# A hybrid conv and forgetting-attention layer in float32 on one core: low parts move from GpSimd to VectorE before the attention, and some small matmuls are queued with a margin

## Chip, cores and metric

The kernel runs on one core of one Trainium2 chip. The metric is the device time of one execution in microseconds (us). Kernels are compared by their medians, runs of both being taken on the same chip.

A core has five engines, each of which works through its own queue in order: TensorE (PE, with its weight loads as PEld), VectorE (DVE), ScalarE (ACT), GpSimd (POOL) and SyncE (SP), which here only issues DMAs.

## The reference

One layer with post-norm is applied to 1024 new prompt tokens and to 32 tokens of a running stream with 512 cached positions; model width 1024. What matters here, cut down:

```
p = x @ w_in                      # GLU pair | q | k | v | forget logits | branch gates
u = a * sigmoid(b)
y = depthwise_causal_conv(u, width 31) + b_dw          # 512 channels
y_conv = silu(layer_norm(y)) @ w_conv_out
logf = log_sigmoid(p_f + b_f);  c = cumsum(logf)
o = softmax(q k / 8 + c_q - c_k, causal) v             # 8 heads of 64
m = sigmoid(g_conv) * y_conv + sigmoid(g_attn) * (o @ w_attn_out)
x1 = layer_norm(alpha * x + m @ w_o)
x2 = layer_norm(alpha * x1 + relu(x1 @ w_up)^2 @ w_down)
```

Everything is float32, and the keys, values, log forget values and last conv inputs are outputs too.

## The kernel before

Features lie on partitions, tokens run along the free axis: 1056 tokens in three chunks of 352. Each float32 operand is split into two float32r tiles: a high part (a copy by ACT, or a cast by DVE) and a low part, the subtraction of the high part from the operand (`tt(lo, a, hi, SUB)`). A float32 product is then three passes on PE: high by high, high by low, low by high. The weights are streamed in tiles of 128 x 1024, loaded in halves (`raw`), and split by `Weights.split`: `whi` on ACT, `wlo` by a subtraction on POOL (on DVE only for the first two halves). Raw halves and split tiles have four buffers each.

The stages up to the attention are: the GLU pairs (8 weight tiles); the values (4 tiles); queries and keys (8 tiles); and the first 6 of 16 gate tiles (`ps_g`, 72 matmuls each). Beside them three background streams run:

- `conv()`: on DVE, four channel tiles `ca` of 128 x 1086, each made by one `TENSOR_SCALAR` and 30 taps (`SCALAR_TENSOR_TENSOR ca<-u,prm,ca`). Then, in three chunks c0 to c2 of 362 tokens, a layer norm over channels in `norm_rows`: `total` adds the four tiles, a matmul with a constant matrix spreads the mean (`ps_mu_c`), DVE subtracts it, ACT squares, `total` adds the squares, a second matmul gives the variance (`ps_var_c`), then a square root, a reciprocal, and per tile `done`: a product with 1/std, a sigmoid (`csig`), a product, a high part on ACT (`csh`) and a low part (`csl`). Both go to DRAM (`s_s`).
- `forget()`: the log sigmoid of the forget logits on small tiles (ending with `logf` and `lfs`), running sums by four matmuls (`ps_cum`) and a transpose (`ps_cumt`).
- `x_stream()`: the inputs.

What sets the order is `Issue`. It keeps a rough clock per engine (`t`) from a cost for every operation, and nothing of it is known to the chip: the order of issue is simply the order of each engine's queue. A stream yields what it waits for, and `service`, called after every group of six matmuls, goes on with a stream when `due(need)` is not after the modelled PE clock. For a list of tiles, `due` is the modelled time at which they stand ready. For taps the need is `("dve", 1500)`: a tap is issued when DVE's modelled clock is less than 1500 ns ahead of PE's. At the end of the stage `I.flush()` issues whatever the streams still hold.

After that the pools of the stage close and those of the attention take their place. `load_head` loads operands of a head (k1, q1, k2, q2, v) over SP's queue; k1 of the first head lies where tiles `ca0` and `ca1` lay. The remaining gates are a filler between the attention's matmuls. Merge, output projection and feed-forward follow.

Of the kernel before, what the change touches and what calls it, by code (L numbers as in the profile page):

```python
# [17 lines left out]
P = 128  # L18
# [37 lines left out]
WARM = 19  # L56
GB = 2
# [21 lines left out]
class Issue:  # L79
    """Issues instructions and keeps a rough clock for each engine. Every engine works in the order of  # L80
    issue, so work that stands ready is put in front of work that would wait: `fill` and `service`."""
# [32 lines left out]
    def due(self, need):  # L114
        if callable(need):
            return 0.0 if need() else 1e12
        if isinstance(need[0], str):
            return max(self.t[e] for e in need[:-1]) - need[-1]
        return max(max(self.ready(a), self.free.get(a.tensor.name, 0.0)) for a in need)
# [19 lines left out]
    def finish(self, last):  # L139
        """issues what is left of a background stream and of those before it in its group"""  # L140
# [11 lines left out]
    def drain(self):  # L152
        """issues all background streams: the oldest that can go on, or else the first that can"""
# [6 lines left out]
    def pick(self, n, bias=0.0):  # L160
        """the engine that would be through with a tensor_tensor first"""
        pool, dve = (max(self.t[e], self.t["pe"] - 500) for e in ("pool", "dve"))
        return "pool" if pool + n * 1.97 + 150 + bias < dve + n * 1.01 + 80 else "dve"
# [74 lines left out]
class Slots:  # L238
    """A tile pool whose slots the clock knows"""
# [24 lines left out]
def hybrid_layer(ctx: ExitStack, tc, io):  # L264
# [15 lines left out]
    # ---- scratch in DRAM  # L280
# [20 lines left out]
    # ---- weights: streamed, split in two float32r parts that add up to the float32 exactly  # L301
# [10 lines left out]
    class Weights:  # L312
        def __init__(self):
            self.raw, self.parts, self.taken, self.done, self.halves = [], [], 0, 0, 0

# [7 lines left out]
        def split(self):  # L323
# [8 lines left out]
            tt(lo, raw, f32(hi), SUB, "dve" if i < 2 else "pool")  # L332
# [26 lines left out]
    def mm3(ps, terms, late=False, low=False):  # L359
        """ps = sum of w.T x over terms; each float32 product as hi hi + hi lo + lo hi"""  # L360
# [17 lines left out]
    # ---- layer norm of one block of tokens, features on the partitions of several tiles: 1/std and  # L378
    # the centred rows in place; a background stream whose steps come when their operands stand ready
# [16 lines left out]
    def norm_rows(pl, psl, tiles, mean, tag, n, s, engs, done):  # L396
        yield [s]
# [9 lines left out]
        yield [s]  # L407
# [7 lines left out]
    # sixteen rows of tiles: the inputs, then what the merge reads, then the residual and hidden units  # L415
# [11 lines left out]
    def gates(tiles, banks, staging, tag, bufs, xh_read=None):  # L427
        """the gates before their sigmoid; xh_read is called with the last tile's products of xh through"""
# [27 lines left out]
    # =============================================================== projections, convolution  # L456
    with pool("conv") as pv_, pool("a") as pa, pool("pa", space=PSUM) as psa:
# [40 lines left out]
        # products of ones, read by nobody, bring the tensor engine to its full clock as the inputs arrive  # L498
# [61 lines left out]
        def conv():  # L560
# [7 lines left out]
            for c in range(3):  # L568
                cs = slice(c * CC, (c + 1) * CC)
                tiles = [ca[j][:, cs] for j in range(NJ)]  # L570
                s = total(pv_, tiles, f"m{c}", CC, ("dve", "dve", "pool", "pool"))

                def done(rstd, c=c, cs=cs, tiles=tiles):
                    for j, y in enumerate(tiles):
# [8 lines left out]
                        tt(lo[:, j, :], y, f32(hi[:, j, :]), SUB, "pool")  # L583
                    for dst, src in ((s_s[0], hi), (s_s[1], lo)):
# [3 lines left out]
                        else:  # L588
# [5 lines left out]
                                     ("dve", "dve", "pool", "pool"), done)  # L594

        # ---- log sigmoid of the forget logits and its running sums
        logf = pa.tile([P, 9, H], F32, name="logf")

        def forget():
# [21 lines left out]
            yield [logf, lfs]  # L621
# [10 lines left out]
            yield [cum]  # L632
# [8 lines left out]
        # the first tiles go chunk by chunk, as the inputs arrive  # L641
# [17 lines left out]
        # ---- values, tokens on partitions  # L659
        for half in range(2):  # L660
            ws = [W.take() for g in range(2)]
            for t in range(9):
# [15 lines left out]
                tt(vs[:r, :, DH:P], vv, f32(vs[:r, :, 0:DH]), SUB, "pool")  # L678
# [12 lines left out]
        # ---- queries (times -1/8) and keys, features on partitions  # L691
        for m in range(4):
            for name in "qk":
                w = W.take()
                for c in range(NCH):
# [7 lines left out]
                    tt(lo, a, f32(hi), SUB, "pool")  # L703
# [23 lines left out]
    # =============================================================== attention, branch gates  # L727
    with pool("b") as pb, pool("pb", space=PSUM) as psb:
# [21 lines left out]
        # the first products of the merge, as the rows of the inputs come free  # L750
# [28 lines left out]
        # operands of one head: [kh; kh] on [qh; ql] and [kl; c, 1] on [qh; 1, -c] add up to all of  # L779
        # -(q k / 8 + c_q - c_k)  # L780
# [17 lines left out]
        # two heads of the running stream: their cached keys and values are split on the chip  # L798
# [87 lines left out]
        class Rows:  # L886
            """128 query rows of one head against their keys"""
# [56 lines left out]
        class Stream:  # L944
            """the new queries of two heads of the running stream against cached and new keys"""
# [93 lines left out]
    # =============================================================== merge, output projection, FFN  # L1039
# [62 lines left out]
    def run_sum(cs, m, s, tag, eng="dve"):  # L1102
        """adds tile m of a block of tokens to the running sum over features"""
# [12 lines left out]
    def squares(sq, t, total, nth, n, tag):  # L1116
        """squares one more tile and adds the square before it to the running sum"""
# [15 lines left out]
    def norm_out(cs, tag, s, emit, need=()):  # L1133
        """layer norm of a block of tokens in place, a background stream as well"""
# [66 lines left out]
    with pool("h") as ph:  # L1201
# [28 lines left out]
        def down_first(wd, cs):  # L1230
            """the first tiles, with what the newest hidden units add put last"""
# [44 lines left out]
        def output(cs, new=False):  # L1276
            """where a block of tokens puts its results: in place, or two tiles at a time"""
# [21 lines left out]
        # the last tokens go through the last hidden units block by block, with the weights kept  # L1299
# [28 lines left out]
        # the last block: the mean over its first tile is taken off as soon as it is known, which leaves  # L1328
# [134 lines left out]
```

## Time and profile before

| | us |
|---|---|
| median of 3 runs | 1587.16 |
| lowest and highest | 1586.59, 1590.54 |
| span of the profiled execution | 1585.9 |
| PE busy in it | 1506.2 |
| DVE, ACT, POOL busy | 911.8, 487.4, 655.2 |

The record of the profiled execution gives its span from the first to the last instruction; what lies around the span is taken as the difference to the median, 1.3 us.

How to read it: slices are 40 equal parts of the span with the busy share in tenths. In rows of groups the numbers behind `|` are busy us and mean ns of one, then the idle time just before and what ended it. In rows in order of time: start, us, engine, line, operation, output<-inputs, shapes, count, and in brackets idle time before and its releaser. In the list of waits: total us, times, longest. `ps_` names a PSUM tile; buffer numbers are left out.

### The profile page before, as it was taken

The page shows a single profiled execution, that of the slowest core. Times are in us where ns is not written, and L with a number is a line of the kernel's source. Part 1 is how long each engine was busy: PE and PEld are TensorE (multiplying, and loading weights), DVE is VectorE, ACT ScalarE, POOL GpSimd, SP SyncE. Part 2 cuts the span into 40 slices and gives each one's busy share as a digit, 9 for nine tenths or more (in the row PEclk, how much of TensorE's full clock was granted, in tenths as well). Part 3 has the DMA queues.
Part 4 walks back from the last instruction along what each step waited for, and adds up shares of the span by engine and source line. Part 5 has one row for each costly group of instructions (what it writes and reads, how often), then busy time and mean ns, then how long its engine had stood idle before and what let it go on. Part 6 is the DMA issues. An engine that isn't in the chain of part 4 may idle for free.

```text
span 1585.9 us, 24681 instructions
## 1 busy us (share of the span) xinstructions
PE 1506.2 (95%) x9524; PEld 1476.5 (93%) x9524; DVE 911.8 (57%) x1385; ACT 487.4 (31%) x1048; POOL 655.2 (41%) x557
## 2 busy tenths in 40 slices
PE   9999598699999999999899999999999999999985
PEld 8999598698989999899899999999999999999984
DVE  4799999653656654864887243333424333342588
ACT  4211211453656655433554121111111111111133
POOL 2436576633445533657765222222222222222346
PEclk9999699899999999999999999999999999999998
DMA  6214443437555557626531111111111111114412
GB/s 199 69 46 137 134 136 125 151 114 219 152 142 147 146 150 269 210 87 190 154 96 54 47 47 41 54 41 50 44 47 47 41 54 41 54 41 140 153 37 73
DMA packets 113731, 165.56 MB, mean 104 GB/s; under 512 B 19146, under 2 KB 71626, under 8 KB 113614
## 3 DMA queue, kind: packets, MB, share of 16 engines
q1 hardware_dynamic: 113614, 163.99, 33.6%
q8 instruction: 75, 1.23, 0.3%
q14 instruction: 42, 0.34, 0.1%
HBM read 120.38 MB, written 43.54 MB: 103 GB/s over the span
## 4 chain that ended last, share of the span: by engine, by line
PE 67%; DVE 7%; issue 2%; ACT 1%; DMA 1%; POOL 1%; SPq 0%; DVEq 0%; ACTq 0%; POOLq 0%
PE ps_dn L202 22%; PE ps_up L202 22%; PE ps_g L202 8%; PE ps_yc L202 3%; PE ps_o L202 2%; PE ps_s L202 2%; PE ps_pv L202 2%; PE ps_tr L206 2%; PE ps_yo L202 2%; DVE acc L231 2%; DVE lnvar_n L223 2%; DVE acc L223 0%; DVE yg L223 0%; DVE rstd_n L235 0%; DMA g_s<-gt 0%
## 5 line engine op out<-in xcount | busy, mean ns | idle before, releaser
L223 POOL TENSOR_TENSOR wlo<-raw,whi 128x512 fp32r<-128x512 f32 (+1 forms) x262 | 381.8, 1478 | 605.6 <-ACT whi L214 598.7
L214 ACT ACTIVATE whi<-raw 128x512 fp32r<-128x512 f32 (+1 forms) x264 | 151.9, 623 | 396.9 <-issue 337.6
L202 PE MATMUL ps_dn<-hh,whi 128*128 128x352 f32 x768 | 249.3, 325 | 0.0
L202 PE MATMUL ps_dn<-hl,whi 128*128 128x352 f32 x768 | 247.8, 323 | 0.8 <-DVE hl L223 0.8
L202 PE MATMUL ps_dn<-hh,wlo 128*128 128x352 f32 x768 | 248.0, 323 | 0.0
L223 DVE TENSOR_TENSOR acc<-ps_dn,acc 128x352 f32<-128x352 f32 x168 | 87.8, 523 | 194.5 <-PE ps_dn L202 194.5
L231 DVE SCALAR_TENSOR_TENSOR ca<-u,prm,ca 128x1086 f32<-128x1086 f32 x120 | 197.7, 1648 | 2.5
L223 DVE TENSOR_TENSOR r<-r 128x352 f32<-128x352 f32 x96 | 52.5, 547 | 184.7 <-ACT r L214 184.7
L202 PEld LDWEIGHTS ps_dn<-hl,whi 128*128 128x128 f32 x768 | 144.5, 188 | 1.3 <-DVE hl L223 1.0
L202 PEld LDWEIGHTS ps_dn<-hh,whi 128*128 128x128 f32 x768 | 144.3, 188 | 0.5 <-DVE acc L223 0.2
L202 PEld LDWEIGHTS ps_dn<-hh,wlo 128*128 128x128 f32 x768 | 144.4, 188 | 0.0
L202 PE MATMUL ps_g<-xh,whi 128*128 128x352 f32 x384 | 132.4, 345 | 0.7 <-ACT gt L214 0.6
L214 ACT ACTIVATE r<-ps_up 128x352 f32<-128x352 f32 x96 | 44.5, 463 | 259.8 <-PE ps_up L202 253.6
L202 PE MATMUL ps_g<-xh,wlo 128*128 128x352 f32 x384 | 124.1, 323 | 0.0
L202 PE MATMUL ps_g<-xl,whi 128*128 128x352 f32 x384 | 121.9, 323 | 0.0
L223 DVE TENSOR_TENSOR hl<-r,hh 128x352 fp32r<-128x352 f32 x96 | 84.0, 875 | 3.3
L223 DVE TENSOR_TENSOR tl<-ps_tr,th 128x512 fp32r<-128x512 f32 (+2 forms) x96 | 51.2, 553 | 57.9 <-ACT th L214 56.0
L202 PE MATMUL ps_up<-x_0h,whi 128*128 128x352 f32 x256 | 82.9, 324 | 0.0
L202 PE MATMUL ps_up<-x_1h,wlo 128*128 128x352 f32 x256 | 82.4, 322 | 0.0
L202 PE MATMUL ps_up<-x_0h,wlo 128*128 128x352 f32 x256 | 82.4, 322 | 0.0
L202 PE MATMUL ps_up<-x_1h,whi 128*128 128x352 f32 x256 | 82.4, 322 | 0.0
L202 PE MATMUL ps_up<-x_0l,whi 128*128 128x352 f32 x256 | 82.3, 322 | 0.0
(283 smaller groups left out, 3834.6 us busy)
## 6 DMA issues: line engine op xcount, KB each, us to landing
raw<-in_w_in_dram SPq DMA_DIRECT2D x64, 256.0 KB
raw<-in_w_up_dram SPq DMA_DIRECT2D x64, 256.0 KB
raw<-in_w_down_dram SPq DMA_DIRECT2D x64, 256.0 KB
raw<-in_w_o_dram SPq DMA_DIRECT2D x48, 256.0 KB
g_s<-gt SPq DMA_DIRECT2D x48, 176.0 KB
yg<-g_s SPq DMA_DIRECT2D x48, 176.0 KB
xr<-in_x_dram SPq DMA_DIRECT2D x12, 352.0 KB
xr<-in_x_dram SPq DMA_DIRECT2D x24, 176.0 KB
```

The costliest lines, as they stand in the source:

```text
L202: self.nc.tensor.matmul(ps, lhsT=w, rhs=x, start=start, stop=stop)
L206: self.nc.tensor.transpose(ps, x, ident)
L214: self.nc.scalar.activation(out, in_, func, **kw)
L223: (self.nc.vector if eng == "dve" else self.nc.gpsimd).tensor_tensor(out, a, b, op)
L231: self.nc.vector.scalar_tensor_tensor(out, a, s, b, op0, op1)
```

## The change

Three things change. Up to the attention all low parts and sums of `total` are made by DVE instead of POOL, which is left with filling constants (memsets); `W.engine` is set back to POOL before the attention. A need may now be `(MARGIN, [tiles])`, which is due 3000 ns of the modelled clock after the tiles stand ready. The two products of each conv norm and the products of the running sums have such needs. Comments are taken out as well.

```
+MARGIN = 3000.0
...
     def due(self, need):
         if callable(need):
             return 0.0 if need() else 1e12
+        if isinstance(need[0], float):
+            return self.due(need[1]) + need[0]
...
     class Weights:
         def __init__(self):
+            self.engine = "dve"
...
-            tt(lo, raw, f32(hi), SUB, "dve" if i < 2 else "pool")
+            tt(lo, raw, f32(hi), SUB, self.engine)
...
     def norm_rows(pl, psl, tiles, mean, tag, n, s, engs, done):
-        yield [s]
+        yield (MARGIN, [s])
         mu = psl(f"mu_{tag}")[:, :n]
         mm(mu, mean, s, True, True)
...
         s = total(pl, sq, f"v{tag}", n, engs)
-        yield [s]
+        yield (MARGIN, [s])
...
-                s = total(pv_, tiles, f"m{c}", CC, ("dve", "dve", "pool", "pool"))
+                s = total(pv_, tiles, f"m{c}", CC, ("dve",) * 4)
...
-                        tt(lo[:, j, :], y, f32(hi[:, j, :]), SUB, "pool")
+                        tt(lo[:, j, :], y, f32(hi[:, j, :]), SUB)
...
-                                     ("dve", "dve", "pool", "pool"), done)
+                                     ("dve",) * 4, done)
...
-            yield [logf, lfs]
+            yield (MARGIN, [logf, lfs])
...
-            yield [cum]
+            yield (MARGIN, [cum])
...
-                tt(vs[:r, :, DH:P], vv, f32(vs[:r, :, 0:DH]), SUB, "pool")
+                tt(vs[:r, :, DH:P], vv, f32(vs[:r, :, 0:DH]), SUB)
...
-                    tt(lo, a, f32(hi), SUB, "pool")
+                    tt(lo, a, f32(hi), SUB)
...
+    W.engine = "pool"
     with pool("b") as pb, pool("pb", space=PSUM) as psb:
```

How the order moves, at two places. The first is PE's queue at the mean product of chunk c1, before, in the middle of the gates (`ps_g1`, `ps_g2`: second and third gate tile; line 202 is the helper that issues matmuls):

```order
L202 MATMUL ps_g1_2_78_2936<-xh7_101,whi21_2480 128x352
L202 MATMUL ps_g1_2_78_2936<-xl7_109,whi21_2480 128x352
L202 MATMUL ps_g1_2_78_2936<-xh7_101,wlo21_2481 128x352
L202 MATMUL ps_mu_c1_79_2974<-lns_dve_m1_2910,mean_c_193 128x362
L202 MATMUL ps_g2_0_80_2993<-xh0_94,whi22_2596 128x352
L202 MATMUL ps_g2_0_80_2993<-xl0_102,whi22_2596 128x352
```

The same product in the changed kernel, on PE at the end of the stage (`ps_g5` is its last gate tile, `ps_g6` the attention's first filler):

```order
L205 MATMUL ps_g5_2_89_3272<-xl7_109,whi25_2885 128x352
L205 MATMUL ps_g5_2_89_3272<-xh7_101,wlo25_2886 128x352
L205 MATMUL ps_mu_c1_91_3347<-lns_dve_m1_3343,mean_c_193 128x362
L205 MATMUL ps_var_c1_92_3365<-lns_dve_vc1_3361,mean_c_193 128x362
L205 MATMUL ps_mu_c2_93_3402<-lns_dve_m2_3398,mean_c_193 128x362
L205 MATMUL ps_var_c2_94_3420<-lns_dve_vc2_3416,mean_c_193 128x362
L205 MATMUL ps_g6_0_3493<-xh0_94,whi26_2986 128x352
```

The mean product of c1 moved from place 1774 of PE's queue to 2062, and the three products after it, which had some 30 to 100 gate matmuls between them, stand directly behind it. The mean product of c0 moved from 1640 to 1994, its variance product from 1671 to 2049, and the first running-sum product from 1131 to 1161.

The second place is DVE's queue in the changed kernel, where the norm of chunk c0 ends and that of c1 begins (line 226 is the helper of subtractions and additions, 234 that of `SCALAR_TENSOR_TENSOR`):

```order
L234 SCALAR_TENSOR_TENSOR ca3_208<-ca3_208,prm_86,rstd_c0_3287 128x362
L234 SCALAR_TENSOR_TENSOR ca3_208<-ca3_208,prm_86,csig0_3_3336 128x362
L226 TENSOR_TENSOR csl0_3320<-ca3_208,csh0_3319 128x362
L226 TENSOR_TENSOR lns_dve_m1_3343<-ca0_205,ca1_206 128x362
L226 TENSOR_TENSOR lns_dve_m1_3343<-lns_dve_m1_3343,ca2_207 128x362
L226 TENSOR_TENSOR lns_dve_m1_3343<-lns_dve_m1_3343,ca3_208 128x362
L226 TENSOR_TENSOR ca0_205<-ca0_205,ps_mu_c1_91_3347 128x362
```

The low part `csl0` and the second and third addition were on POOL before, beside DVE's queue; now they stand in it, ahead of the subtraction of the mean.

## The prediction

> **What bounds the kernel now.** I read the page first, then the list of what TensorE (PE) waits for up to 420 us, then stretches of 20 us.
>
> ```profile
> span 1585.9 us, 24681 instructions
> ...
> PE 1506.2 (95%) x9524; PEld 1476.5 (93%) x9524; DVE 911.8 (57%) x1385; ACT 487.4 (31%) x1048; POOL 655.2 (41%) x557
> ...
> PE   9999598699999999999899999999999999999985
> ...
> PEclk9999699899999999999999999999999999999998
> ```
>
> PE is busy for 95% of the span; its holes stand in slices 5, 7 and 8 of 40, all before the attention, and the granted clock drops there too. Nearly all of the idle time has two owners (us in total, times, longest), with one more row at the attention's first scores:
>
> ```profile
> PE ps_mu_c L202 <- DVE lns_dve_m L223: 19.6, 2, 18.4
> PE ps_cum L202 <- DVE lfs L218: 19.4, 1, 19.4
> PE ps_s L202 <- DMA q<-qh_s: 1.9, 1, 1.9
> ```
> ```profile
> 186.50 0.66 PE L202 MATMUL ps_cum<-logf,cst 128*128 128x64 f32 x2 [19.43 <-DVE lfs L218]
> 290.02 1.54 PE L202 MATMUL ps_mu_c<-lns_dve_m,mean_c 128*128 128x362 f32 x2 [18.40 <-DVE lns_dve_m L223]
> ```
> ```profile
> 180.00:200.00 20.00, 13.50 (x66) 13.51 (x67) 18.86 (x46) 3.35 (x8) 11.06 (x7) 0.65 0.47 153
> 240.00:260.00 20.00, 20.00 (x127) 20.00 (x127) 19.79 (x15) 4.41 (x9) 13.03 (x7) 1.00 0.38 134
> 280.00:300.00 20.00, 9.98 (x50) 9.25 (x51) 13.92 (x16) 7.02 (x12) 11.94 (x9) 0.68 0.43 145
> ```
>
> The columns of the stretches are length, then busy time and count of PE, PEld, DVE, ACT, POOL, then clock. At full clock 127 products fill 20 us: 0.1575 us each. After the first hole 66 take 13.50 us instead of 10.4, after the second 50 take 9.98 instead of 7.9: restarting cost 3.1 + 2.1 = 5.2 us. So the two waits cost 19.4 + 18.4 + 5.2 = 43.0 us. VectorE (DVE) is full in between: it is late, not slow to start.
>
> [...]
>
> **Part 1: low parts and sums move from GpSimd (POOL) to DVE.** The columns are busy us, mean ns, idle before.
>
> ```profile
> L231 DVE SCALAR_TENSOR_TENSOR ca<-u,prm,ca 128x1086 f32<-128x1086 f32 x120 | 197.7, 1648 | 2.5
> L223 POOL TENSOR_TENSOR wlo<-raw,whi 128x512 fp32r<-128x512 f32 x51 | 81.4, 1618 | 59.2 <-ACT whi L214 53.4 <-DMA s_s<-csl 5.8
> L223 POOL TENSOR_TENSOR vs<-v,vs 128x256 fp32r<-128x256 f32 x16 | 28.4, 1775 | 28.5 <-DVE vs L218 28.5
> L223 POOL TENSOR_TENSOR kl<-k,kh 128x352 fp32r<-128x352 f32 x12 | 22.7, 1894 | 17.2 <-DVE kh L218 14.9 <-DMA out_k_dram<-k 2.3
> L223 DVE TENSOR_TENSOR wlo<-raw,whi 128x512 fp32r<-128x512 f32 x2 | 1.4, 693 | 4.2 <-ACT whi L214 4.2
> ```
> ```profile
> L231 DVE SCALAR_TENSOR_TENSOR ca<-u,prm,ca x120: 1331/1351/6685, 50.9 to 286.0; 128x1086 f32<-128x1086 f32 x120
> 291.60 1.86 DVE L223 TENSOR_TENSOR ca<-ca,ps_mu_c 128x362 f32<-128x362 f32 x4 [1.48 <-PE ps_mu_c L202]
> ```
> ```profile
> 49.10 1.72 DVE L227 TENSOR_SCALAR ca<-u,prm 128x1086 f32<-128x1086 f32 x1
> ```
> ```profile
> L218 DVE CAST kh<-k 128x352 fp32r<-128x352 f32 x12 | 7.2, 603 | 0.0
> ```
>
> A convolution tap has a minimum of 1331 ns, a median of 1351 and a mean of 1648: some are stretched, up to 6685. The POOL subtractions run beside them, and I take those as the cause. Without them the taps give back 120 x (1.648 - 1.351) = 35.6 us. What DVE takes over: 362 columns cost 1.86 / 4 = 0.465 us and 512 cost 0.69, so about 54 weight halves at 0.69 = 37 us, 18 of v at 0.33 (256/362 of 0.465) = 6, 24 of q and k at 0.45 = 11, 12 of the convolution's output at 0.465 = 6, and one more addition in each of six sums = 3: 63 us. Bounds for DVE's balance: +63 if the stretch has another cause, below nothing if nearly all its other work was stretched as well; I take the difference, +27.
>
> That is off the path if DVE reaches the two products in time. Counting the order from the convolution's first operation at 49.1 to its first sum: 120 taps x 1.351 = 162; 44 weight halves x 0.69 = 30; low parts of v, q and k 17; their 42 casts at no more than 0.60 = 25; some 50 small operations of the GLU, the forget logits and the sums, 16 by an estimate of 0.3 each from the rows above. End at 49 + 250 = 299 at the latest.
>
> When does PE ask? In the trace PE stood before the first mean product from 290.0 - 18.4 = 271.6; without the first wait and its restart that is 271.6 - 19.4 - 3.1 = 249.1. The order puts this product at row 1994 instead of 1640: 354 x 0.1575 = 55.8 later, at 305. So this wait goes, with 6 us to spare. The running sums' product moves 30 rows, from 167.1 (186.5 - 19.4) to 171.8. Its inputs begin when the last v tile is done, 84 rows before the old place, at 153.9; behind it stand four weight halves (2.8), one tap, a cast pair and the short logarithm chain (about 6): ready near 166. This wait goes too, with 5 us to spare. **Gain: 43 us**, at the end of the projections.
>
> **Part 2: the margin moves the conv norm past its cover.** Later products have less projection work behind them. In the order the first variance product stands 12 gate products before the end of the block (row 2049 of 2061). The products for means and variances of chunks 1 and 2 are rows 2062 to 2065, one behind the other: the flush at the block's end issues all that is left. PE can only wait. In the trace the same chain had 300 gate products between its steps. Its price comes from the trace's own steps:
>
> ```profile
> 300.70 0.60 DVE L231 SCALAR_TENSOR_TENSOR ca<-ca,prm,rstd_c 128x362 f32<-128x362 f32 x1
> 301.96 0.60 DVE L231 SCALAR_TENSOR_TENSOR ca<-ca,prm,csig 128x362 f32<-128x362 f32 x1 [0.67 <-ACT csig L214]
> 302.47 0.59 DVE L231 SCALAR_TENSOR_TENSOR ca<-ca,prm,rstd_c 128x362 f32<-128x362 f32 x1
> ...
> 338.85 1.86 DVE L223 TENSOR_TENSOR ca<-ca,ps_mu_c 128x362 f32<-128x362 f32 x4 [0.97 <-PE ps_mu_c L202]
> ...
> 345.58 2.42 DVE L235 RECIPROCAL rstd_c<-rstd_c 128x362 f32<-128x362 f32 x1 [1.63 <-ACT rstd_c L214]
> 348.03 0.60 DVE L231 SCALAR_TENSOR_TENSOR ca<-ca,prm,rstd_c 128x362 f32<-128x362 f32 x1
> 350.63 0.60 DVE L231 SCALAR_TENSOR_TENSOR ca<-ca,prm,csig 128x362 f32<-128x362 f32 x1 [2.00 <-ACT csig L214]
> ```
> ```profile
> 339.41 1.85 ACT L214 ACTIVATE sq_c<-ca 128x362 f32<-128x362 f32 x4 [3.36 <-DVE ca L223]
> 344.98 0.56 ACT L214 ACTIVATE rstd_c<-ps_var_c,eps 128x362 f32<-128x362 f32 x1 [1.03 <-PE ps_var_c L202]
> ```
> ```profile
> 303.18 0.96 POOL L223 TENSOR_TENSOR csl<-ca,csh 128x362 fp32r<-128x362 f32 x1 [8.06 <-ACT csh L214]
> ...
> 359.61 0.82 POOL L223 TENSOR_TENSOR csl<-ca,csh 128x362 fp32r<-128x362 f32 x1
> ```
>
> One tile: 1.26 from its first product to its second (301.96 - 300.70), 1.22 on to the low part's start (303.18 - 301.96), and 0.465 for that on DVE, where the next tile now stands behind it: 2.95. Four tiles are 11.8; in chunks 1 and 2 the table load before the first sigmoid adds 1.3 (350.63 - 348.03 = 2.60 against 1.26), so 13.1. From a chunk's end to the next reciprocal's end: three additions 1.5, mean product 1.0, subtraction and squares 2.4 (338.85 to 341.26), last addition 0.6, variance product 1.0, square root 0.6, reciprocal 2.4: 9.5.
>
> PE ends its last gate at 249.1 + 421 x 0.1575 + 1.6 (two products) = 317.0. The first reciprocal ends by 318.5 (variance product at 314.7, 3.8 on), and a weight pair that waits for that last gate stands behind it: the four tiles start at 320. Chunk 0 ends at 331.8, chunk 1 at 331.8 + 9.5 + 13.1 = 354.4, the third reciprocal at 363.9, and its variance product 3.1 earlier (344.9 against 348.0): 360.8. **PE stands still for 317.0 to 360.8, 43.8 us**, which is what it gained. Chunk 2 ends at 363.9 + 13.1 = 377.0.
>
> **Part 3: the first head's loads.** Their tiles lie where the convolution's lay, and on SP's queue they stand behind its stores.
>
> ```profile
> 361.14 2.00 SPq L197 DMA_DIRECT2D s_s<-csl  x2
> 363.23 3.04 SPq L197 DMA_DIRECT2D g_s<-gt  x3
> 367.54 1.58 SPq L197 DMA_DIRECT2D raw<-in_w_in_dram  x2
> 369.21 0.53 SPq L197 DMA_DIRECT2D k<-kh_s  x1
> ...
> 377.51 0.84 SPq L197 DMA_DIRECT2D g_s<-gt  x2
> ```
> ```profile
> 382.30 0.30 PE L202 MATMUL ps_s<-k,q 128*128 128x128 f32 x1 [1.91 <-DMA q<-qh_s]
> 383.63 0.46 ACT L214 ACTIVATE gt<-ps_g 128x352 f32<-128x352 f32 x1 [9.45 <-DMA g_s<-gt]
> ```
>
> The chain of chunk 2 ended at 360.4, its store was issued by 363.1 (2.7 on), then gate stores and weight loads came first; from the first load to scores took 13.1. In the new order the gate stores and weight loads are ahead of the convolution's stores, so loads start at 377.0 + 2.7 = 379.7 and scores at 392.8. PE has 102 gate products (16 us) for those 32 us, and the last six wait for a copy that waits for a gate store behind the loads: 14.4 after the first load (383.63 - 369.21), so 394.1, and with copy and products 395.5. Bounds 392.8 and 395.5; I take 395, because both orders hold that store behind the loads.
>
> **Sum.** Scores at 395 instead of 382.3: +12.7. By then PE has done 12 gate products more (row 2168 instead of 2156): -1.9. It restarts cold: 2.1 to 3.1 in the rows above, nothing if the gate products before kept it warm; I take +2. Together +12.8. From there the instructions are the same. The span goes from 1585.9 to 1598.7; the median of the runs stands 1.3 over that span, so **1600**.
>
> **Rivals.** A measurement tells 0.3% (4.8 us) from no change.
> - *Slower as summed* (0.55): 1593 to 1608, from start errors of 3 us, chain errors of 4 and the bounds of the loads.
> - *Faster: the norm chain shrinks in the flush* (0.11). DVE alone, with no gate copies and weight halves between, could overlap the low part of a tile with the next one's sigmoid: 1.77 per tile as when POOL did it (302.47 was the next start) instead of 2.95, on 12 tiles 14 us, and 4 more if the loads land sooner: 1600 - 18 = 1582. Against it: the order has the low part between. It decides from scores before 377.
> - *No change* (0.17): half of that, or the loads not held by the chain: 1583 to 1591, about 1587.
> - *Slower by more: DVE's queue delays weights or q and k* (0.12). Weight halves now wait behind taps in one queue; four of them stall PE 2.5 us each if DVE runs 10 us late: 1610. Against it: 6 us to spare above, and the halves are split some tiles ahead. For it: DVE has 98% in the row for 240 to 260 us.
> - *The change doesn't do what it says* (0.05): taps stay stretched, the running sums' wait stays with 19.4 - 4.7 = 15 us: 1615.
>
> Chances: slower 0.55 + 0.12 + 0.05 = 0.72, same 0.17, faster 0.11. The range takes in most of both sides: 1583 to 1613.
>
> **What would show it.** Right: taps near 1351 ns mean; no PE wait for the log forget values; PE waiting over 35 us for the sums and squares of the convolution at 315 to 365; first scores near 395. Wrong: waits for weight low parts; the flush under 30 us; scores before 385.

## The result and the profile after

The changed kernel takes 1603.44 us (median; 1602.33 to 1603.62), the kernel before 1587.16. The ratio is 1.0095, 95% interval 1.0081 to 1.0109: slower by 16 us. The profiled span grew from 1585.9 to 1601.8, by 15.9.

The page of the changed kernel (span, busy times, then TensorE's slices and granted clock):

```profile
span 1601.8 us, 24674 instructions
...
PE 1510.6 (94%) x9524; PEld 1479.6 (92%) x9524; DVE 915.3 (57%) x1503; ACT 488.9 (31%) x1048; POOL 467.1 (29%) x439
...
PE   9999999916999999999989999999999999999985
...
PEclk9999999957999999999999999999999999999997
```

The holes in slices 5, 7 and 8 are gone, and a deeper one stands in slices 9 and 10. Its owners, in the list of TensorE's waits up to 440 us:

```profile
PE ps_mu_c L205 <- DVE lns_dve_m L226: 33.6, 2, 17.9
PE ps_g L205 <- ACT gt L217: 12.5, 2, 8.4
PE ps_var_c L205 <- DVE lns_dve_vc L226: 7.4, 2, 3.7
```

The forget logits' wait of 19.4 us is in no row any more. The taps in the tile view (minimum, median, maximum in ns, first and last start):

```profile
L234 DVE SCALAR_TENSOR_TENSOR ca<-u,prm,ca x120: 1342/1350/1354, 51.1 to 297.9; 128x1086 f32<-128x1086 f32 x120
```

The first product of the running sums in the same view of its own tile, and the first mean product in order of time:

```profile
L205 PE MATMUL ps_cum<-logf,cst x2: 217/246/274, 171.9 to 171.9; 128*128 128x64 f32 x2
```
```profile
305.05 0.77 PE L205 MATMUL ps_mu_c<-lns_dve_m,mean_c 128*128 128x362 f32 x2
```

No tap is stretched (the maximum was 6685 before), and neither product waits. The whole loss stands in the flush. Stretches of 20 us, with the columns that the prediction named:

```profile
320.00:340.00 20.00, 3.12 (x4) 1.00 (x4) 10.96 (x21) 7.87 (x14) 0.00 (x0) 0.50 0.28 98
340.00:360.00 20.00, 1.54 (x2) 0.50 (x2) 11.59 (x19) 6.28 (x11) 0.00 (x0) 0.50 0.20 72
360.00:380.00 20.00, 12.29 (x50) 10.93 (x50) 11.09 (x18) 9.13 (x16) 0.37 (x1) 0.67 0.01 3
```

In 40 us TensorE does six passes, of three products, at a granted clock of 0.50 (half clock; below, a TensorE in this state is called cold). VectorE's rows in order of time show the chain that it waits for:

```profile
334.33 1.86 DVE L226 TENSOR_TENSOR ca<-ca,ps_mu_c 128x362 f32<-128x362 f32 x4 [1.73 <-PE ps_mu_c L205]
...
340.18 2.42 DVE L238 RECIPROCAL rstd_c<-rstd_c 128x362 f32<-128x362 f32 x1 [2.26 <-ACT rstd_c L217]
...
346.40 0.54 DVE L226 TENSOR_TENSOR csl<-ca,csh 128x362 fp32r<-128x362 f32 x1 [0.57 <-ACT csh L217]
346.85 0.59 DVE L234 SCALAR_TENSOR_TENSOR ca<-ca,prm,rstd_c 128x362 f32<-128x362 f32 x1
...
349.28 0.54 DVE L226 TENSOR_TENSOR csl<-ca,csh 128x362 fp32r<-128x362 f32 x1 [0.57 <-ACT csh L217]
```

A tile takes 349.28 - 346.40 = 2.88 us. The last low part starts at 379.8, the gate copy ahead of the first scores at 397.28 (`397.28 0.46 ACT L217 ACTIVATE gt<-ps_g`, behind a gate store), the first scores at 399.4 instead of 382.3. From there nothing is lost: the last product of the feed-forward starts at 1580.2 instead of 1564.55, 15.65 later against 17.1 at the scores.

### The profile page after: what moved, and what is told of

The parts are those of the page before. It is cut to its first block, busy times and chain, and to the rows that moved or that the text cites. A ratio compares the mean times of both kernels' runs of the same rounds, so it can differ in the third digit from the quotient of the medians.

```text
span 1601.8 us, 24674 instructions
## 1 busy us (share of the span) xinstructions
PE 1510.6 (94%) x9524; PEld 1479.6 (92%) x9524; DVE 915.3 (57%) x1503; ACT 488.9 (31%) x1048; POOL 467.1 (29%) x439
## 4 chain that ended last, share of the span: by engine, by line
PE 84%; DVE 9%; ACT 2%; issue 2%; DMA 1%; SPq 1%; POOL 0%; DVEq 0%; ACTq 0%; POOLq 0%
PE ps_dn L205 22%; PE ps_up L205 21%; PE ps_g L205 11%; PE ps_v L205 3%; PE ps_glub L205 3%; PE ps_yc L205 3%; PE ps_k L205 3%; PE ps_glua L205 3%; PE ps_q L205 3%; PE ps_o L205 2%; PE ps_s L205 2%; PE ps_pv L205 2%; PE ps_tr L209 2%; PE ps_yo L205 2%; DVE acc L234 2%
## 5 line engine op out<-in xcount | busy, mean ns | idle before, releaser
L226 POOL TENSOR_TENSOR wlo<-raw,whi 128x512 fp32r<-128x512 f32 x204 | 285.8, 1422 | 544.4 <-ACT whi L217 540.7
L217 ACT ACTIVATE whi<-raw 128x512 fp32r<-128x512 f32 (+1 forms) x264 | 152.0, 624 | 397.0 <-issue 318.4
L205 PE MATMUL ps_dn<-hh,whi 128*128 128x352 f32 x768 | 249.5, 325 | 0.0
L205 PE MATMUL ps_dn<-hl,whi 128*128 128x352 f32 x768 | 248.1, 323 | 0.4 <-DVE hl L226 0.4
L205 PE MATMUL ps_dn<-hh,wlo 128*128 128x352 f32 x768 | 248.1, 323 | 0.0
L234 DVE SCALAR_TENSOR_TENSOR ca<-u,prm,ca 128x1086 f32<-128x1086 f32 x120 | 161.8, 1348 | 2.4
L205 PE MATMUL ps_g<-xh,whi 128*128 128x352 f32 x384 | 133.5, 348 | 13.1 <-ACT gt L217 12.5
L205 PEld LDWEIGHTS ps_dn<-hl,whi 128*128 128x128 f32 x768 | 144.6, 188 | 1.0 <-DVE hl L226 0.6
L205 PEld LDWEIGHTS ps_dn<-hh,whi 128*128 128x128 f32 x768 | 144.4, 188 | 0.5
L205 PEld LDWEIGHTS ps_dn<-hh,wlo 128*128 128x128 f32 x768 | 144.4, 188 | 0.0
L205 PE MATMUL ps_g<-xh,wlo 128*128 128x352 f32 x384 | 126.1, 328 | 0.0
L205 PE MATMUL ps_g<-xl,whi 128*128 128x352 f32 x384 | 123.9, 328 | 0.0
L217 ACT ACTIVATE r<-ps_up 128x352 f32<-128x352 f32 x96 | 44.4, 463 | 259.8 <-PE ps_up L205 253.6
L205 PEld LDWEIGHTS ps_g<-xh,whi 128*128 128x128 f32 x384 | 74.8, 195 | 15.0 <-ACT gt L217 13.0
L226 DVE TENSOR_TENSOR tl<-ps_tr,th 128x512 fp32r<-128x512 f32 (+2 forms) x96 | 51.2, 553 | 58.1 <-ACT th L217 57.3
L205 PE MATMUL ps_up<-x_0h,whi 128*128 128x352 f32 x256 | 83.0, 324 | 0.0
L205 PE MATMUL ps_up<-x_1h,wlo 128*128 128x352 f32 x256 | 82.5, 322 | 0.0
L205 PE MATMUL ps_up<-x_0h,wlo 128*128 128x352 f32 x256 | 82.5, 322 | 0.0
```

The source lines that it names most:

```text
L205: self.nc.tensor.matmul(ps, lhsT=w, rhs=x, start=start, stop=stop)
L217: self.nc.scalar.activation(out, in_, func, **kw)
L226: (self.nc.vector if eng == "dve" else self.nc.gpsimd).tensor_tensor(out, a, b, op)
L234: self.nc.vector.scalar_tensor_tensor(out, a, s, b, op0, op1)
```

## The experiments

Every time below is compared with the kernel before on the same chip (medians of 1589.4 to 1590.5 us); ratios are to it. Nothing is left out of the computation in any of them. First scores are counted from the first product whose loads are all there: in the kernel before that is the second score product, 2.1 us behind the first.

### The margin or the move: changing one at a time

The margin taken out of the changed kernel:

```
-MARGIN = 3000.0
+MARGIN = 0.0
```

> The changed kernel with the margin set to 0, so only the move from GpSimd to VectorE is left. In its order the mean and variance products of chunks 1 and 2 still stand one behind the other after the last gate; the first running-sum product is at place 1143 of TensorE's queue (1161 with the margin), the mean product of chunk 0 at 1976 (1994). Theory A, the move itself fills VectorE's queue, so that the taps end later against the gates and the norm is left without cover: no wait at the running sums (asked for near 169, ready near 167), the same 44 us of idle time at the end of the projections, 1600 to 1605. Theory B, as the prediction put it, the margin moves the norm past its cover: the idle time at the end goes and the two waits stay away, 1545 to 1565.

Measured: 1597.86 us, ratio 1.0048 (1.0032 to 1.0064). The list of waits:

```profile
PE ps_mu_c L205 <- DVE lns_dve_m L226: 27.8, 2, 17.8
PE ps_g L205 <- ACT gt L217: 15.0, 2, 10.9
PE ps_var_c L205 <- DVE lns_dve_vc L226: 7.4, 2, 3.7
```

The four products stand one behind the other at rows 2062 to 2065 without any margin. So the stacking comes from the work moved to VectorE: the order's clock for VectorE runs later, and with it the time at which sums are taken to be due. The margin alone adds some 6 us (33.6 instead of 27.8 in the first row). TensorE does not wait for the running sums or the first mean here either, so the margin bought nothing. Theory A held in its mechanism; its time (1600 to 1605) was 2 us too high.

The other half, the kernel before with the margins alone:

```
+        if isinstance(need[0], float):
+            return self.due(need[1]) + need[0]
...
-        yield [s]
+        yield (MARGIN, [s])
```

> The kernel before with the margin of 3000 alone; low parts and sums stay on GpSimd. The running-sum product is 18 places later, the mean product of chunk 0 24 places, that of chunk 2 114 places, and the last variance product stands right behind the last gate. Theory A: both waits stay, near 16 and 17 us, since VectorE is as late as before and 3 us of margin cover little; taps stay stretched (mean near 1650 ns); the last chunk of the norm ends some 15 us later and the first scores with it, near 393 us, so 1592 to 1599. Theory B (the margin removes the waits and exposes the norm): waits under 5 us, 44 us of idle time at the end, 1600 or more.

Measured: 1599.04, ratio 1.0053 (1.0037 to 1.0069).

```profile
PE ps_mu_c L205 <- DVE lns_dve_m L226: 19.4, 1, 19.4
PE ps_cum L205 <- DVE lfs L221: 16.5, 1, 16.5
PE ps_g L205 <- ACT gt L217: 12.9, 2, 7.7
```

Both old waits stay, and a third comes at the gate copies ahead of the scores (first scores at 395.2): 3 us of margin are too few against sums that come 16 to 19 us late, and the later chain is paid for.

### More gates ahead of the attention as a cover

The changed kernel with more gate tiles ahead of the flush, ten and twelve instead of six:

```
-GA = 6
+GA = 10
```

> The changed kernel with 10 gate tiles ahead of the attention instead of 6 (6 left as its filler instead of 10): 288 more matmuls between the first variance product and the flush. Theory A: the norm of chunk 1 is covered, some 5 us are left at the last two products and some 15 us before the first scores; those come near 403 us with 300 matmuls (47 us) more done than at the 382.3 us of the kernel before, so 26 us less: near 1562. Rival C, the loss of the changed kernel does not come from the missing cover: no change, 1600 to 1605. Rival D, the attention then lacks filler and gives it back: first scores as said, but the attention ends 20 us or more later in matmuls done: 1580 or more.

> The changed kernel with 12 gate tiles ahead of the attention. In its order the last variance product stands 50 or more matmuls ahead of the end of the projections. Theory A: no idle time over 3 us at the four products and little before the first scores, which come near 401 us with 438 matmuls (69 us) more done than in the kernel before: 50 us less, near 1540, if the attention can do with 4 gate tiles as filler. Rival C: 1600 to 1605. Rival D: the attention is short of filler, TensorE waits there for softmax parts, and more than 20 us come back: 1560 to 1590.

Measured: 1612.81, ratio 1.0143 (1.0126 to 1.0160), and 1615.72, ratio 1.0154 (1.0131 to 1.0178). The cover works at its place: with ten gates 4.8 us are left at the variance products, with twelve nothing. But the scores start at 406.4 and 409.2, and the attention then misses its filler: rival D, at a higher price than it was given for twelve gates (1560 to 1590). The largest of TensorE's waits after 340 us, with ten gates and with twelve:

```profile
PE ps_tr L209 <- ACT ob L217: 19.7, 15, 8.3
```
```profile
PE ps_pv L205 <- DVE tl L226: 14.1, 16, 2.0
```

The useful reading lies in the lengths. From first scores to the last value product (`ps_pv`) the attention took 241 us in the kernel before (382.3 to 623.4), 240 in the changed one (399.4 to 639.2), and 241 with ten gates and with twelve. It gets no shorter when four or six of the ten gate tiles inside it are taken out, so they cost nothing there. Ahead of it a gate costs its time, less what it fills of TensorE's waits: with four more tiles the scores came 7 us later. So the end of the kernel follows the start of the first scores; the next runs go for that.

### The serial low part

```
-                        tt(lo[:, j, :], y, f32(hi[:, j, :]), SUB)
+                        tt(lo[:, j, :], y, f32(hi[:, j, :]), SUB, "pool")
```

> The changed kernel with one edit: the low part of the conv norm's output goes back to GpSimd, the margins and all else stay. Theory (the tail of the conv norm is a serial chain of twelve tiles on VectorE, and the subtraction of the low part is a step of it): a tile of the norm takes 1.9 to 2.0 us instead of 2.88 to 2.94, twelve tiles give 11 to 12 us back, the chain ends near 370 instead of 380.4, the first scores come near 388 instead of 399.4 and the time is near 1592 (1589 to 1596). Rival (the chain is bound by the cold products and the reciprocals, and the low part lies beside them): the scores stay at 398 to 400 and the time at 1601 to 1604.

Measured: 1593.39, ratio 1.0028 (1.0017 to 1.0038), scores at 389.3. Giving the twelve low parts of the conv norm back to GpSimd takes 10 of the 16 us away: on VectorE each of them stood between one tile and the next. With the 6 us of the margin that would be the whole loss; no run takes out both and leaves the rest.

### What stretches the taps

The kernel before with the weights' low parts alone on VectorE:

```
-            tt(lo, raw, f32(hi), SUB, "dve" if i < 2 else "pool")
+            tt(lo, raw, f32(hi), SUB, self.engine)
```

> The kernel before with one edit: the low parts of the weights are made on VectorE up to the attention; the low parts of v, q, k and of the conv norm stay on GpSimd, and there is no margin. Theory (a tap is stretched by a GpSimd subtraction that runs beside it, and by nothing else): the taps' mean falls from 1648 ns to about 1.51 us, since only the stretches beside v, q and k are left; the wait of TensorE for the sums of log forget (16.5 to 18.4 before) is gone or under 4. Time 1580 to 1600. Rival (the stretch comes from VectorE's own queue or from the loads): the mean stays at 1.62 or more.

Measured: 1582.60, ratio 0.9958 (0.9943 to 0.9973). The group of the taps, then the wait for the running sums:

```profile
L231 DVE SCALAR_TENSOR_TENSOR ca<-u,prm,ca 128x1086 f32<-128x1086 f32 x120 | 174.0, 1450 | 2.5
```
```profile
PE ps_cum L202 <- DVE lfs L218: 4.2, 1, 4.2
```

Time as expected, the taps a little better (1.51 was expected) and the wait at the bound. The mean goes from 1648 to 1450 with the weights moved, and in the changed kernel to 1348 with v, q, k and the norm moved as well. In these runs the stretch follows GpSimd's subtractions. In the records of the kernel before, 92 taps with a GpSimd subtraction beside them take 1.739 us on average and 28 without take 1.348, none over 1.352. How a subtraction on GpSimd slows a tap on VectorE is not shown.

This part of the change alone makes the kernel faster by 7 us; the rest of it, in the conv norm above all, turned the gain into a loss.

### The norm's chain in another order

The conv norm of the changed kernel written anew, all else as it was: sums of all three chunks, three mean products together, three variance products together, three reciprocals, and tiles so that the next tile's scale stands ahead of the last tile's low part.

```
+            s = sums(ca, "m")
+            yield (MARGIN, s)
+            for c in range(3):
+                mm(mu[c], mean_c, s[c], True, True)
...
+            s = sums(u, "v")
+            yield (MARGIN, s)
+            for c in range(3):
+                mm(var[c], mean_c, s[c], True, True)
...
+                    late.append((second, third))
+                    if len(late) > 1:
+                        late[-2][0]()
+                    if len(late) > 2:
+                        late.pop(0)[1]()
```

`second` is the product with the sigmoid and the high part, `third` the low part and its stores.

> The changed kernel with its conv norm written in another order, the margins kept: the sums of all three chunks first, then the three mean products one behind the other, the three variance products likewise, and the twelve tiles' steps so that the next tile's scale stands ahead of the last tile's low part on VectorE. Theory (the time lost is the twelve tiles' serial chain and the products that each chunk waits for alone behind the gates): two waits for products instead of four, the tiles at 1.3 to 1.5 us of VectorE each, the chain ends near 351 instead of 380.4, first scores at 367 to 372 instead of 399.4 and the time near 1573 (1568 to 1580). Rival 1 (the attention is held by something else, its loads or the low parts of k and q, and starts at 385 or later whatever the norm does): 1588 to 1600. Rival 2 (the attention's 240 us from first scores to its last value product grow when it starts earlier, since its 240 us hold gates that no longer fit): scores at 370, time 1585 or more.

Measured: 1571.53, ratio 0.9894 (0.9879 to 0.9908). The theory held, the scores 1 us and the chain's end 6 us earlier than it said: no wait for a product is over 1.0 us, the chain ends at 344.8, scores start at 366.0. What is left is a wait for gate copies (26.5 us in total). The same kernel without margins, and then with the casts of v, q and k moved to ScalarE too:

```
-MARGIN = 3000.0
+MARGIN = 0.0
```

> The grouped conv norm without margins, the casts of v, q and k left on VectorE. It tells which of the two edits of the 1553 us kernel brought its 18.5 us over the grouped norm with margins. Theory (VectorE is behind by the casts, and the margins hold nothing in the grouped norm, whose products waited 1.0 us at most): the three mean products stand at rows 1994 to 1996 instead of 1868 to 1870, the last gate before the variance products is as late as with the margins, first scores at 363 to 367, the time 1568 to 1573. Rival (the margins held the products back): first scores at 350 or earlier, the time 1552 to 1558.

```
-                cp(vs[:r, :, 0:DH], vv)
+                act(vs[:r, :, 0:DH], vv, AF.Copy)
...
-                    cp(hi, a)
+                    act(hi, a, AF.Copy)
```

> The grouped conv norm without margins, and the casts of v, q and k to their high part on ScalarE instead of VectorE, so that all of the norm's products are queued among the gates. Theory (the end is set by when the first scores start, and the attention takes 240 us from there whatever the filler): no wait of TensorE over 5 us at the norm's products, first scores at 335 to 345 instead of 399.4, the time 1540 to 1552. Rival 1 (the loads of the conv heads' k behind the chain, or the planner's order, hold the scores at 360 or later): 1563 to 1580. Rival 2 (the attention slows when less lies ahead of it): first scores at 340, but 1565 or more.

Measured: 1572.09, ratio 0.9885 (0.9873 to 0.9898), and 1552.99, ratio 0.9773 (0.9759 to 0.9788). So the margins are worth nothing in the grouped norm, and the casts brought the 19 us. With 42 casts less, the order puts the mean products at rows 1868 to 1870 instead of 1994 and the variance products at 1937 to 1939 instead of 2063; the chain ends at 326.5, beside gates, and the scores start at 347.7. VectorE's rows in order of time in this kernel:

```profile
310.77 0.59 DVE L234 SCALAR_TENSOR_TENSOR ca<-ca,prm,rstd_c 128x362 f32<-128x362 f32 x1
311.28 0.59 DVE L234 SCALAR_TENSOR_TENSOR ca<-ca,prm,csig 128x362 f32<-128x362 f32 x1
311.78 0.53 DVE L226 TENSOR_TENSOR ca<-ca,u 128x362 fp32r<-128x362 f32 x1
312.23 0.59 DVE L234 SCALAR_TENSOR_TENSOR ca<-ca,prm,rstd_c 128x362 f32<-128x362 f32 x1
```

A tile is 312.23 - 310.77 = 1.46 us of VectorE with no idle time, against 2.88 in the changed kernel, for the same three operations. The attention took 240.3 us from 366.0 and 240.4 from 347.7: the whole gain at the scores reached the end. This version is faster than both kernels, by 36 us than the one before. The forecast of 1540 to 1552 was missed by 1 us, because the scores came 3 to 13 us later than forecast, behind the next wait.

### The last wait ahead of the scores

That wait: `PE ps_g L205 <- ACT gt L217: 12.1, 3, 10.0`, for a gate copy whose buffer waits for a store behind the heads' loads.

```
-GB = 2
+GB = 3
```

> The 1553 us kernel (grouped norm, no margins, casts on ScalarE) with three buffers instead of two for a gate's output. In it TensorE waits 10.4 us (335.4 to 345.8) ahead of the first scores for a gate's copy, and that for a store of a gate behind the heads' loads on SP's queue. Theory (the start of the scores is held by that buffer alone by then): the wait is gone, the first scores come at 338 to 341 instead of 347.7 and the time is 1543 to 1547. Rival (the conv heads' low parts, ready at 333 to 340, or the next gate's buffer hold them): 1550 to 1554.

Measured: 1563.03, ratio 0.9828 (0.9814 to 0.9842): 10 us slower than with two buffers. Both theories are wrong. The waits up to 440 us:

```profile
PE ps_tr L209 <- DVE tl L226: 4.3, 1, 4.3
PE ps_s L205 <- DMA q<-ql_s: 4.2, 1, 4.2
PE ps_s L205 <- DMA q<-c_s: 2.2, 1, 2.2
```

The 10 us are gone and the head's own loads become the wait. The first score product starts at 342.5, and the next one waits for a load:

```profile
345.20 0.45 PE L205 MATMUL ps_s<-k,q 128*128 128x128 f32 x1 [2.25 <-DMA q<-c_s]
```

So the scores start at 345.2, only 2.5 earlier, and from there the attention takes 254 us instead of 240. Counted over the same number of products, most of the added time stands in steps of 5.8, 4.7 and 2.0 us, the first two at waits of 4.3 and 2.8 us for a transpose's operand with slower products behind them (granted clock 0.96 from 420 to 500 and 0.97 from 500 to 560). The third buffer also changes the order of the filler; whether that or the earlier loads open the stalls isn't settled.

### The clock in the flush

The changed kernel with products that nobody reads, in TensorE's idle time: 14 behind each tile of chunks 0 and 1, 8 behind each of the last two mean products, three behind squares, 24 behind chunk 1's variance product.

```
+        var = psl(f"var_{tag}")[:, :n] if keep else None
         mm(mu, mean, s, True, True)
+        if keep:
+            busy(var, 8)
...
+                        for _ in range(14 if c < 2 else 0):
+                            nc.tensor.matmul(mu, lhsT=hi[:, j, :P], rhs=hi[:, j, :], start=True, stop=True)
```

> The changed kernel with matrix products added whose results nobody reads, all in the wait of TensorE between the last gate and the last variance product: 14 behind each tile of chunks 0 and 1, and some behind each mean product and behind chunk 1's variance product, so that TensorE does not stand still there. Theory (the conv chain is 3.4 us longer than forecast because its mean and variance products are made at half the clock): granted clock near 1.0 instead of 0.50 in the stretch from 320 to 360, from the mean product's start to its first reader 1.0 us instead of 1.73, from a variance product to the reciprocal 1.6 instead of 2.26, the chain's last low part at 376 to 378 instead of 380.4, first scores at 393 to 397 and the time 1596 to 1600. Rival (the 1.73 us are the latency behind an idle engine, not the clock, or the added products stand in the way): chain's end at 380 or later, 1602 to 1607.

Measured: 1602.51, ratio 1.0076 (1.0062 to 1.0090) beside 1.0095 without them: no difference that counts. Its forecast of 1596 to 1600 was missed; the time lies where the rival put it. At its place the theory held in part. Two stretches of this kernel, then in order of time the last mean product, its first reader and the last reciprocal, of this kernel and below of the changed one:

```profile
320.00:340.00 20.00, 18.26 (x98) 16.05 (x98) 12.70 (x21) 7.10 (x13) 0.00 (x0) 0.88 0.21 76
340.00:360.00 20.00, 14.88 (x73) 13.52 (x73) 11.62 (x23) 8.80 (x14) 0.00 (x0) 0.83 0.21 74
```
```profile
355.51 0.77 PE L205 MATMUL ps_mu_c<-lns_dve_m,mean_c 128*128 128x362 f32 x2
356.32 1.86 DVE L226 TENSOR_TENSOR ca<-ca,ps_mu_c 128x362 f32<-128x362 f32 x4 [1.55 <-PE ps_mu_c L205]
361.47 2.42 DVE L238 RECIPROCAL rstd_c<-rstd_c 128x362 f32<-128x362 f32 x1 [1.56 <-ACT rstd_c L217]
```
```profile
357.41 1.54 PE L205 MATMUL ps_mu_c<-lns_dve_m,mean_c 128*128 128x362 f32 x2 [17.86 <-DVE lns_dve_m L226]
359.00 1.86 DVE L226 TENSOR_TENSOR ca<-ca,ps_mu_c 128x362 f32<-128x362 f32 x4 [1.73 <-PE ps_mu_c L205]
364.84 2.42 DVE L238 RECIPROCAL rstd_c<-rstd_c 128x362 f32<-128x362 f32 x1 [2.26 <-ACT rstd_c L217]
```

From the product's start to its reader it is 0.81 instead of 1.59 us, and the reciprocal's wait 1.56 instead of 2.26: that the cold clock lengthens these steps is shown (the product's two passes take 0.77 us, at a granted clock of 0.83 from 340 to 360, instead of 1.54 at 0.50). (The subtraction's idle time falls only to 1.55, not to the 1.0 of the forecast, since the added products themselves stand ahead of the mean product, and the clock came to 0.83 to 0.88, not 1.0.) The last low part starts at 376.4 instead of 379.8, though 1.6 of that come from an earlier start of the chain (first scale at 317.7 instead of 319.3), and the scores at 395.5, 3.8 earlier. Then the attention gives 2.6 us back, at two places: its first 20 us go at a clock of 0.87 (0.93 in the changed kernel), and 20 us around a wait for a transpose's operand differ too. First this kernel, then the changed one:

```profile
455.00:475.00 20.00, 18.15 (x115) 16.84 (x114) 14.01 (x24) 12.20 (x27) 12.44 (x15) 0.91 0.51 138
```
```profile
459.00:479.00 20.00, 18.14 (x124) 17.18 (x123) 13.91 (x24) 11.52 (x26) 12.13 (x15) 1.00 0.49 146
```

Both stretches hold the same wait of 1.9 us; the clock drops in the one and not in the other. Over 420 to 500, where the wait lies, it is 0.98 in this kernel and 1.00 in the kernel before, the changed one, the one without the margin and the grouped norm. In the records of the kernel before and of the changed one the granted clock changes only after whole steps of 3.41 us (the 51.2 us at half clock in the flush are 15 of them). In both the wait falls across two steps, with 0.16 and 1.71 us in those of the kernel before and 0.97 and 0.89 in those of the changed one, and the clock stays at 1.00. Each of the 12 steps at full clock in these two records in which TensorE was idle for 2.15 us or more is followed by a step at half clock; of the others only the first of each record is (1.19 and 1.73 us idle). The drop to 0.91 over 20 us is as much as one step at half clock would make (1 - 3.41 / 2 / 20, an estimate). Where the wait falls on the steps in the kernel kept busy is not shown, and no run moves a pause on purpose.

### Is the move to VectorE needed?

The kernel before, with its taps and low parts as they were, the grouped norm (low part on GpSimd), the casts on ScalarE and a margin of 20 us:

```
+MARGIN = 20000.0
...
-                cp(vs[:r, :, 0:DH], vv)
+                act(vs[:r, :, 0:DH], vv, AF.Copy)
...
+                        tt(lo, y, f32(hi), SUB, "pool")
```

> The kernel before, with its low parts and so its slowed taps on GpSimd as they were, and with three edits: the conv norm in the grouped order (its low part on GpSimd), the casts of v, q and k on ScalarE, and a margin of 20 us (not 3) on the products for the running sums and the conv means. It asks whether the move of the low parts is needed at all. Theory (what counts is that no product is asked before its sums and none so late that the norm's chain passes the gates; the slow taps cost VectorE time that nobody waits for then): taps' mean still 1.6 us, the four products of the running sums at row 1275, the mean products at rows 1748 to 1750 and the variance products at 1949 to 1951, no wait over 6 us at any of them, first scores at 345 to 352, the time 1550 to 1560, as the 1553 us kernel. Rival (the move to VectorE is what carries the gain, since with slow taps the norm's sums come after 300): waits of 10 us or more at the mean products, first scores at 360 or later, 1565 to 1585.

Measured: 1586.40, ratio 0.9975 (0.9965 to 0.9985). My theory falls, and the rival is nearer: the scores start at 381.4, after its 360, though its waits were put higher and its time 1 us lower.

```profile
L234 DVE SCALAR_TENSOR_TENSOR ca<-u,prm,ca 128x1086 f32<-128x1086 f32 x120 | 210.6, 1755 | 3.9
```
```profile
PE ps_g L205 <- ACT gt L217: 15.3, 2, 10.1
PE ps_k L205 <- DVE pre L667: 9.3, 1, 9.3
PE ps_mu_c L205 <- DVE lns_m L226: 6.0, 2, 4.0
```

The taps are slower still (1755 ns), the norm's first scale comes at 334.4 instead of 303.9 in the 1553 us kernel, and the products that were put off are waited for again. So, in this order, the move of the low parts was worth having: it needed the chain behind it to be rebuilt. No other margin was tried with the low parts left on GpSimd.

## Why the prediction was right, point by point

- **The gain of 43 us** came as said. Taps took 1348 ns on average (1351 was said); the running sums' product starts at 171.89 (171.8 was said) and the mean product at 305.05 (305 was said), both without a wait.
- **VectorE's balance, "+27"**, was mis-sized, off the path. Its busy time up to the first scores grew by 4.5 us only (292.3 to 296.8). What it took over cost about what was said (60 weight halves took 41 us), but more than the taps had been stretched: the 42 casts of v, q and k fell from 22 to 13 us and `z<-zt,prm` from 5.6 to 0.2. The first sum was still ready only at 300.8, past the "299 at the latest", so 4 of the 6 us to spare were left.
- **Two readings of the lines** were off and changed nothing: the row of granted clock is lower in slices 5 and 8, not in 7, and VectorE has 99% (19.79 of 20) in the row for 240 to 260 us, not 98.
- **The cause of the stretch**, taken from overlap alone, is shown by moving parts of it: 1648, 1450, 1348.
- **The stall in the flush**: said 317.0 to 360.8, 43.8 us; measured 317.0 to 364.2, 47.2, of which 41.0 are idle (33.6 + 7.4 in the list of waits) and the rest the four products. A tile said at 2.95, measured at 2.88 to 2.94.
- **The mis-sized term** is "from a chunk's end to the next reciprocal's end ... 9.5", which used 1.0 us for each product from a trace in which TensorE was warm (granted clock 1.00 from 320 to 360). It measured 11.7 (chunk 2's first addition begins at 355.6, its reciprocal ends at 367.3). The cold clock (0.50) makes an estimated 1.4 of the 2.2 (1.73 and 2.26 instead of 1.0 and 1.63); most of the rest lies in the subtraction, the squares and their sums, which took 3.6 instead of the 3.0 put down. Over two chunks that is 4.3, less 0.9 by which chunk 0 was early: the chain ended at 380.4 instead of 377.0.
- **The loads**: the first load was issued 2.2 us behind the chain instead of 2.7, and from it to the scores took 16.8 instead of 15.3. With the 3.4 above, scores at 399.4 instead of 395. From the scores on, the changed kernel's span was 1.2 us shorter, where the sum had nothing (-1.9 + 2). Together 15.9 instead of 12.8, and 1603.4 instead of 1600.
- **The attribution was wrong.** Part 2 is headed "the margin moves the conv norm past its cover". Without the margin the products of chunks 1 and 2 stand in the same rows (1597.86 us): the move of work to VectorE puts them there, and the margin accounts for some 6 us. The sum was right because the rows of the order, not their cause, went into it.
- **The rival "faster: the norm chain shrinks in the flush"** named a real possibility, but not in this order. The grouped norm made it true by writing the low part behind the next tile's scale: 1.46 us a tile.
- **The other rivals** did not occur: no wait for a low part of a weight stands in the list ("DVE's queue delays weights or q and k"), the taps are not stretched ("the change doesn't do what it says"), and the loads were held by the chain ("no change").

## What to carry to other kernels

When a transfer of work frees one wait, look for the last serial chain behind it and count what still lies beside that chain: here 43 us were gained in the projections and lost in a flush with nothing beside it, and the same move with the chain rebuilt and the casts moved to ScalarE (1553 us) beat the kernel before by 36. Price an operation in a chain by rows in which its engine is in the state that it will be in: products on a TensorE that stood still took 1.59 us instead of 0.81. In this kernel a filler inside the attention was free and the same filler ahead of it was not, so the start of the first scores is the number to watch; it did not tell the end in the kernel with a third gate buffer, whose filler stands in another order.

## What was not expected of the hardware

The attention took 239.5 to 242.5 us in thirteen of the kernels here whatever lay ahead of it, and 254 in the one with a third gate buffer. And a wait of the same 1.9 us cost no clock in the kernel before and the changed one (1.00 in the 20 us around it) and some in the kernel kept busy (0.91); what tells them apart is not shown.
